# A transformer layer on one core: each feed-forward weight's rounding queued behind the evictions of the product just ended

## The chip, the cores and the metric

The kernel runs on one core of one Trainium2 chip. The metric is the device time of one execution in microseconds (us), here the median of several runs. A core has four engines that compute and that each work through a queue of their own, in order: TensorE (PE in the profile, with its weight loads as PEld), VectorE (DVE), ScalarE (ACT) and GpSimd (POOL). SyncE (SP), ACT and POOL also issue DMAs. [...]

## The reference, cut to what matters

The reference is one trunk layer for 640 tokens (128 of context, 512 of a latent grid) with 1024 features: adaLN modulation, two attentions, a gated merge, then a feed-forward, then a last norm. All of it is float32. The change lies in the feed-forward alone:

```
h2 = rmsnorm(x, n2) * (1 + sc2) + sh2
x  = x + g2 * (square(relu(h2 @ w1)) @ w2)      # w1: 1024 x 4096, w2: 4096 x 1024
y  = rmsnorm(x, final_norm_g)
```

## The kernel before, in words

**Number format.** PE multiplies in fp32r, a rounded float32. To keep the precision, an operand is split into a rounded part (hi) and the rest (lo), and a product of two operands is three matmuls: hi by hi, hi by lo, lo by hi. Making hi and lo from a float32 weight is what the change calls the weight's rounding.

**Feed-forward.** Features lie on the partitions, tokens on the free axis. The 4096 hidden features are taken in four chunks (c = 0 to 3). Each layer of a chunk is a 2 by 2 block product, which is done with seven block products in place of eight (a scheme of the Strassen kind, named A11, A12, S3, S2, A22, S1, S4). Layer 1 of chunk 0 is done plainly before. What is left is the list SEQ (line 1368) of 196 products, which the loop at line 1665 goes through. Here they are numbered 0 to 195: chunk 0 has 0 to 27 (layer 2 only), chunk 1 has 28 to 83, chunk 2 has 84 to 139, chunk 3 has 140 to 195. In chunks 1 to 3 the first 26 products are layer 1, then layer 2 follows with two layer-1 products left among it. One product is twelve matmuls of 128x128 by 128x320 (lines 1679 to 1681; only line 1681 reads the lo half of the weight) into one PSUM bank of eight. A12 accumulates onto the bank of A11, and S1 and S4 onto that of S2, after the earlier content has been read.

**After each product** come its evictions (`layer1`, line 1507, and `layer2`, line 1579). In layer 1: ACT copies A11 (line 1510); DVE adds or subtracts S3, A22, S2, S1 and S4 (lines 1514 to 1524); after A12, S2, S1 and S4 ACT does relu and square (lines 1504, 1505), for the last three on what DVE has just written. In layer 2 DVE adds the gated product to the residual `x` (line 1532, in one or two token pieces), after an ACT copy for A11 (lines 1583, 1593). In chunk 3 `done_half` follows for the halves that are then complete: ACT squares `x` (line 1547), DVE adds the square to a sum (line 1551), ACT scales `x` by the last norm's gain (line 1552). When all eight blocks of a half are done, the last norm follows (lines 1559 to 1569) with the output DMAs. Besides there is the work between the layers: `operand` (lines 1482 to 1489) rounds the hidden activations into hi (ACT) and lo (DVE), and `t_raw` (lines 1491 to 1501, DVE) forms their sums and differences.

**Weights.** `Operands.feed` (line 1387) loads a float32 weight pair into a staging buffer, through the SP queue (line 1398). There are three buffers for the A products (`wst`) and four for the others (`wsb`), and the latter get a second weight block added by an accumulating DMA from the POOL queue (line 1401). `Operands.conv` (line 1409) is the rounding of the next product's weight: hi by ACT (line 1416), lo by DVE (line 1421; by POOL for A12 and A22 of layer 1; for the four S4 of chunk 3 by an ACT copy of -hi, line 1418, and an accumulating DMA from POOL, line 1419). After S3, S2 and A22 it has POOL add the next block into the same staging half (line 1424); after A12 and S4 the staging buffer is free and `feed` loads the next into it. `wb` has six buffers, three each under two tags in turn, so a weight's rounding can start when the product six places before it has ended. `ahead` (line 1432) calls `conv` at the end of each product's code, so the weight of product i+6 is rounded in the code of product i.

**Order.** The program is traced in the order of the code. A list scheduler then lays down each engine's queue: at each step it takes, of the instructions that are ready by its own reckoning, the one traced first. So the rounding for product i+6, traced after the evictions of product i, can still be laid ahead of them where it is ready sooner. The queues so laid are fixed: on the chip an instruction that waits holds up all behind it.

Of the kernel before, what the change touches and what calls it, by code (L numbers as in the profile page):

```python
# [74 lines left out]
def trunk_layer(ctx: ExitStack, tc: tile.TileContext, xT, small_in, wmodA, wmodB, tabs, cacheK, cacheV, bias,  # L75
                w_in, w_br, w_out, w1, w2, yT, akT, avT, bkT, bvT):
    nc = tc.nc
    PE, ACT, DVE = nc.tensor, nc.scalar, nc.vector
# [154 lines left out]
    def flush_later(todo=None):  # L233
        todo = later if todo is None else todo
        n = len(todo)
        for f in todo[:n]:
            f()
        del todo[:n]

    class Weights:  # L240
        def __init__(self):
            self.order = list(w_order())
            self.pos = {k: i for i, (k, _) in enumerate(self.order)}
            self.st, self.t = {}, {}
            self.nd = self.nc = self.live = self.busy = 0
            self.extra = self.defer = False
            self.behind = None
# [51 lines left out]
        def ahead(self):  # L299
            while self.nc < len(self.order):  # L300
                key = self.order[self.nc][0]
                if key in EXTRA and self.extra:
                    return
                if key not in EXTRA and self.live + 2 > 6:
                    return
                self.conv()
            if OPS:
                OPS[0].ahead()

    OPS = []  # L310
# [1059 lines left out]
    class Operands:  # L1370


        def __init__(self):
            self.st = {}
            self.loads = []
            for l, c, n, o in SEQ:
                k = (l, c, n, "A" if o in ("A11", "A12") else "B")
                if k not in self.loads:
                    self.loads.append(k)
            self.t = {}  # L1380
            self.nl = self.nc = 0
            self.busy = {"A": 0, "B": 0}

        def src(self, l, c, n, e):
            return (w1[8 * c + 2 * n + e] if l == 1 else w2[c, 2 * n + e]).rearrange("p (k n) -> p k n", k=KT)
# [46 lines left out]
        def ahead(self):  # L1432
            self.feed()
            while self.nc < len(SEQ) and W.live < 6 and (SEQ[self.nc][0], *SEQ[self.nc][1:3],
                                                         "A" if SEQ[self.nc][3] in ("A11", "A12") else "B") in self.st:
                self.conv()

        def get(self, x):
            while x not in self.t:
# [5 lines left out]
    def bank():  # L1445
        return pp8[0].tile([P, 512], F32, tag="b", bufs=8, name="b")[:, :HT]
# [22 lines left out]
    def opd(c, name):  # L1469
        if (c, name) not in OPD:  # L1470
            OPD[c, name] = (bp[0].tile([P, 8, HT], F32R, tag="op3", bufs=1, name="op") if len(OPD) % 3 == 2 else
                            m.tile([P, 8, HT], F32R, tag="op", bufs=2, name="op"))
        return OPD[c, name]
# [6 lines left out]
    def operand(c, name, ks=slice(0, 4)):  # L1480

        t, src = opd(c, name), hid_raw(c, {"B11": 11, "B21": 21, "T4": 21, "N22": 22}.get(name, 12))[:, ks]
        hi, lo = t[:, ks], t[:, 4 + ks.start:4 + ks.stop]
        if name == "N22":
            ACT.activation(hi, src, AF.Copy, scale=-1.0)
            DVE.scalar_tensor_tensor(lo, src, -1.0, r32(hi), op0=OP.mult, op1=OP.subtract)
        else:
            ACT.activation(hi, src, AF.Copy)  # L1488
            DVE.tensor_sub(lo, src, r32(hi))  # L1489

    def t_raw(c, name, ks=slice(0, 4)):

        b11, b12, b21, b22 = (hid_raw(c, b)[:, ks] for b in (11, 12, 21, 22))
        if name == "T3":
            DVE.tensor_sub(b12, b22, b12)
        elif name == "T2":
            DVE.tensor_add(b12, b12, b11)
        elif name == "T4":
            DVE.tensor_sub(b21, b21, b12)
        else:  # L1500
            DVE.tensor_sub(b12, b22, b12)
# [72 lines left out]
    def fold(n):  # L1574

        for h in range(2):
            gate_half(2 * n + 1, WS[n], h, neg)
# [58 lines left out]
    for n, h in todo:  # L1636
# [7 lines left out]
        e, i = n % 2, n // 2  # L1644
# [20 lines left out]
    for x in SEQ:  # L1665
        l, c, n, o = x
        w = OPS[0].get(x)
        if l == 1:
            xk = XN[o]
        else:  # L1670
            s = opd(c, XOF[o])
            xk = lambda k, s=s: (s[:, k], s[:, 4 + k])
        p = pairs.setdefault((l, c, n), Pair())
        whole = {"A12": "A11", "S1": "S2", "S4": "S2"}.get(o)
        b = getattr(p, "b" + whole) if whole else bank()
        setattr(p, "b" + o, b)
        for k in range(4):
            xh, xl = xk(k)
            PE.matmul(b, w[:, k], xh, start=not whole and k == 0, stop=False, skip_group_check=True)  # L1679
            PE.matmul(b, w[:, k], xl, start=False, stop=False, skip_group_check=True)  # L1680
            PE.matmul(b, w[:, 4 + k], xh, start=False, stop=o not in ("A11", "S2", "S1") and k == 3, skip_group_check=True)  # L1681
        (layer1 if l == 1 else layer2)(c, n, o, b, p)
        W.live -= 1
        if l == 1 and o in ("A12", "S2") and n > 1:
            operand(c, "B11" if o == "A12" else "B21", slice(0, 3) if n == 2 else slice(3, 4))
        if l == 1 and o == "S2":
            fold(n)
        if l == 1 and o == "S4" and n > 1:
            t_raw(c, "T3", slice(0, 3) if n == 2 else slice(3, 4))
        if l == 2:  # L1690
            if (o, n) == ("A11", 2):
                operand(c, "T3")
                t_raw(c, "T2")
                t_raw(c, "T4")
            if (o, n) == ("A11", 3):
                operand(c, "T4")
            if (o, n) == ("A12", 3):
                operand(c, "T2")
                t_raw(c, "T1")
            if (o, n) == ("S3", 3):  # L1700
                operand(c, "T1")
            if (o, n) == ("S2", 3):
                operand(c, "N22")
        OPS[0].ahead()
        flush_later()
        if side:
            side.pop(0)()
# [104 lines left out]
```

## Time and profile before

| | |
|---|---|
| median of 3 runs | 917.87 us (917.49, 917.87, 919.94) |
| the profiled execution's own time | 917.51 us |
| its span, first to last instruction | 915.7 us |
| DVE busy | 713.5 us, 78% of the span |
| ACT busy | 564.8 us, 62% |
| POOL busy | 197.0 us, 22% |
| granted TensorE clock, mean | 0.997 |

A row of a timeline has: start in us, duration in us, engine, line, operation, what it writes and reads, and in square brackets the idle time of the engine ahead of it with what ended it. A row of waits has: engine, what waited, `<-` what it waited for, then us in total, how many times, and the longest. A row of a table of windows has: the stretch, its length, then busy us of PE, PEld, DVE, ACT and POOL with the numbers of instructions, then the granted clock, the DMA share and GB/s. The chain of work that ended last has: start, duration, what.

### The profile page before, as it was taken

The numbers are of one execution on the slowest core, as the hardware profiler recorded it, in microseconds if no ns is written. First come the engines' busy times: TensorE is split into PE (matmuls) and PEld (weight loads), VectorE is DVE, ScalarE is ACT, GpSimd is POOL, SyncE is SP. The second block draws the span as 40 slices with busy tenths as digits, with TensorE's granted clock in tenths as the row PEclk, the third lists the DMA queues.
The fourth block names the chain that finished last, engine by engine and source line by source line (L and its number), as shares of the span: only waits on it lengthen the run. The fifth ranks groups of instructions, "written<-read, shape, count | busy, mean of one in ns | idle before, by whom it ended". The sixth has DMA issues, their size and how long they took to land.

```text
span 915.7 us, 16620 instructions
## 1 busy us (share of the span) xinstructions
PE 901.5 (98%) x6120; PEld 871.5 (95%) x6120; DVE 713.5 (78%) x1508; ACT 564.8 (62%) x1176; POOL 197.0 (22%) x226
## 2 busy tenths in 40 slices
PE   9999999999999999999999999999999999999996
PEld 7799989999999999999999999999999999999995
DVE  6776887757666796767789996995798769976897
ACT  4566777756667765765325667537753576357765
POOL 0020200001211011211120000354244532454140
PEclk9999999999999999999999999999999999999998
DMA  9892400126645398999743463898778876898475
GB/s 348 317 266 69 113 24 26 62 72 159 161 119 125 120 284 256 249 268 251 251 140 100 116 165 105 134 210 186 186 122 191 178 174 144 180 173 182 97 126 151
DMA packets 54465, 151.09 MB, mean 165 GB/s; under 512 B 6704, under 2 KB 10432, under 8 KB 54384
## 3 DMA queue, kind: packets, MB, share of 16 engines
q1 hardware_dynamic: 31440, 99.74, 33.1%
q0 software_dynamic: 21792, 48.98, 30.8%
q10 hardware_dynamic: 1152, 1.31, 0.4%
q8 instruction: 48, 0.79, 0.4%
q14 instruction: 33, 0.27, 0.1%
HBM read 137.67 MB, written 4.60 MB: 155 GB/s over the span
## 4 chain that ended last, share of the span: by engine, by line
PE 81%; DVE 6%; DMA 5%; ACT 4%; issue 2%; POOL 0%; SPq 0%; DVEq 0%; ACTq 0%; POOLq 0%
PE b L1680 10%; PE b L1679 10%; PE b L1681 10%; PE pg L320 7%; PE pg L321 7%; PE pg L322 7%; PE pss L322 4%; PE pss L321 4%; PE pss L320 4%; DMA wsb<-w 2%; PE pt L321 2%; PE pt L322 2%; PE pt L320 2%; DMA ms<-wmodA 2%; PE pt L710 1%
## 5 line engine op out<-in xcount | busy, mean ns | idle before, releaser
L1416 ACT ACTIVATE wb<-wsb 128x512 fp32r<-128x512 f32 x140 | 87.1, 628 | 90.6 <-PE b L1681 59.2
L1680 PE MATMUL b<-op,wb 128*128 128x320 f32 x448 | 138.6, 309 | 0.7 <-DVE op L1489 0.7
L1679 PE MATMUL b<-op,wb 128*128 128x320 f32 x448 | 138.6, 309 | 0.0
L1681 PE MATMUL b<-op,wb 128*128 128x320 f32 x448 | 138.4, 309 | 0.0
L1421 DVE TENSOR_TENSOR wb<-wsb,wb 128x512 fp32r<-128x512 f32 x124 | 92.5, 749 | 26.5 <-ACT wb L1416 26.3
L1424 POOL DMA_DIRECT2D wsb<-w x84 | 74.4, 922 | 127.8 <-DVE wb L1421 99.7
L1123 DVE SCALAR_TENSOR_TENSOR mt<-wmt,cb 128x512 f32<-128x512 f32 x128 | 80.9, 686 | 6.0 <-DMA wmt<-wmodB 6.0
L1680 PEld LDWEIGHTS b<-op,wb 128*128 128x128 f32 x448 | 84.1, 188 | 1.2 <-DVE op L1489 1.2
L1679 PEld LDWEIGHTS b<-op,wb 128*128 128x128 f32 x448 | 84.1, 188 | 0.5 <-DVE x L1532 0.4
L1681 PEld LDWEIGHTS b<-op,wb 128*128 128x128 f32 x448 | 84.1, 188 | 0.0
L272 ACT ACTIVATE wh<-wst 128x512 fp32r<-128x512 f32 (+1 forms) x84 | 61.1, 739 | 32.1 <-PE pg L321 16.6
L1401 POOL DMA_DIRECT2D wsb<-w x28 | 26.0, 930 | 138.0 <-DVE xm L341 41.5
L281 DVE TENSOR_TENSOR wl<-wst,wh 128x512 fp32r<-128x512 f32 (+1 forms) x53 | 43.3, 821 | 14.9 <-ACT wh L272 12.8
L648 DVE TENSOR_TENSOR pl<-pt,ph 128x512 fp32r<-128x512 f32 (+1 forms) x72 | 44.9, 627 | 11.8 <-ACT ph L647 11.2
L647 ACT ACTIVATE ph<-pt 128x512 fp32r<-128x512 f32 (+1 forms) x72 | 39.2, 548 | 15.7 <-PE po L718 4.7
L1532 DVE SCALAR_TENSOR_TENSOR x<-b,parts,x 128x128 f32<-128x128 f32 (+1 forms) x116 | 46.3, 429 | 2.9 <-PE b L1681 2.2
L1416 ACT ACTIVATE wb<-wst 128x512 fp32r<-128x512 f32 x56 | 34.9, 626 | 17.1 <-PE b L1681 10.3
L1679 PE MATMUL b<-t,wb 128*128 128x320 f32 x144 | 44.7, 310 | 0.0
L1681 PE MATMUL b<-t,wb 128*128 128x320 f32 x144 | 44.5, 309 | 0.0
L1680 PE MATMUL b<-t,wb 128*128 128x320 f32 x144 | 44.5, 309 | 0.0
L1489 DVE TENSOR_TENSOR op<-hid,op 128x1280 fp32r<-128x1280 f32 (+2 forms) x32 | 37.0, 1155 | 7.6 <-ACT op L1488 7.4
L1532 DVE SCALAR_TENSOR_TENSOR x<-tp,parts,x 128x320 f32<-128x320 f32 (+2 forms) x60 | 38.9, 677 | 1.0 <-ACT tp L1583 1.0
(890 smaller groups left out, 3009.2 us busy)
## 6 DMA issues: line engine op xcount, KB each, us to landing
wsb<-w POOLq DMA_DIRECT2D x112, 256.0 KB, 5.1
wst<-w SPq DMA_DIRECT2D x36, 512.0 KB, 3.9
wmt<-wmodB SPq DMA_DIRECT2D x32, 512.0 KB, 5.5
wst<-w_in SPq DMA_DIRECT2D x31, 512.0 KB, 4.4
wsb<-w SPq DMA_DIRECT2D x28, 512.0 KB, 4.0
ms<-wmodA SPq DMA_DIRECT2D x16, 512.0 KB, 8.2
wl<-w_in POOLq DMA_DIRECT2D x10, 512.0 KB, 7.6
wst<-w_br SPq DMA_DIRECT2D x8, 512.0 KB, 4.2
```

What stands on the lines that cost most here:

```text
L272: ACT.activation(hi[:, ks], st[:, ks], AF.Copy)
L320: PE.matmul(ps, wh[:, k], xh[:, sl], start=first, stop=False)
L321: PE.matmul(ps, wh[:, k], xl[:, sl], start=False, stop=False)
L322: PE.matmul(ps, wl[:, k], xh[:, sl], start=False, stop=last)
L1123: DVE.scalar_tensor_tensor(t, st[:, q * 512:(q + 1) * 512], 1.0, r32(cb[2 * q + i][:, :512]), op0=OP.mult, op1=OP.mult, accum_out=parts[:, ...
L1416: ACT.activation(w[:, 0:4], t, AF.Copy)
L1421: (nc.gpsimd if o in BLKPOOL[l - 1] else DVE).tensor_sub(w[:, 4:8], t, r32(w[:, 0:4]))
L1424: nc.gpsimd.dma_start(t, self.src(l, c, n, e)[:, 4 * half:4 * half + 4], accum_op=OP.add)
L1532: DVE.scalar_tensor_tensor(X1[i][:, sl], src[:, sl.start - off:sl.stop - off], g[:, j:j + 1], X1[i][:, sl], op0=OP.mult, op1=OP.add)
L1679: PE.matmul(b, w[:, k], xh, start=not whole and k == 0, stop=False, skip_group_check=True)
L1680: PE.matmul(b, w[:, k], xl, start=False, stop=False, skip_group_check=True)
L1681: PE.matmul(b, w[:, 4 + k], xh, start=False, stop=o not in ("A11", "S2", "S1") and k == 3, skip_group_check=True)
```

## The change

After the evictions of each product the loop notes the last instruction traced so far on ACT and the last on DVE. When `ahead` then rounds a weight, each of its ACT instructions is queued behind the noted ACT instruction, and each of its DVE instructions behind the noted DVE instruction. These are bounds on the order in the queue and no waits. Instructions on POOL and SP get no such bound. Products whose evictions have no ACT instruction note an older one. The roundings are traced where they were, six products ahead; the first six are traced ahead of the loop and have no bound.

```diff
@@ class Operands, __init__
             self.busy = {"A": 0, "B": 0}
+            self.behind = []
@@ ahead
-                self.conv()
+                with ExitStack() as order:
+                    for i in self.behind:
+                        order.enter_context(tc.issue_after(i))
+                    self.conv()
@@ the loop over SEQ
         (layer1 if l == 1 else layer2)(c, n, o, b, p)
+        OPS[0].behind = [next(i for i in reversed(nc.cur_bb.bb.instructions) if i.engine == e.engine) for e in (ACT, DVE)]
         W.live -= 1
```

## The prediction

> **What bounds the kernel now.** I read the page first, then a table of windows over the feed-forward, then what PE waited for, then the timelines of PE, ACT and DVE around each wait and at the end.
>
> ```profile
> span 915.7 us, 16620 instructions
> PE 901.5 (98%) x6120; PEld 871.5 (95%) x6120; DVE 713.5 (78%) x1508; ACT 564.8 (62%) x1176; POOL 197.0 (22%) x226
> ```
> ```profile
> 713.00:766.00 53.00, 52.57 (x359) 52.31 (x358) 37.63 (x61) 36.75 (x73) 19.31 (x19) 1.00 0.77 182
> 859.00:906.00 47.00, 47.00 (x316) 46.27 (x315) 44.83 (x84) 35.53 (x66) 13.86 (x16) 1.00 0.57 94
> ```
>
> PE is busy for 98% of the span, at the full granted clock. The first window is layer 1 of chunk 2: 359 matmuls in 52.57 us are 0.146 us each, so a product of twelve takes 1.76 us. The second is layer 2 of chunk 3: DVE is busy 44.83 of 47 us (95%) and has hardly any room. So only the places where PE stands still can be won. In the feed-forward these are few:
>
> ```profile
> PEld b L1679 <- DVE tp L1518: 0.5, 2, 0.3
> ```
> ```profile
> 752.47 0.31 PE L1679 MATMUL b<-op,wb 128*128 128x320 f32 x1
> 753.21 0.42 PE L1680 MATMUL b<-op,wb 128*128 128x320 f32 x1 [0.43 <-DVE op L1489]
> 753.46 0.31 PE L1681 MATMUL b<-op,wb 128*128 128x320 f32 x1
> ...
> 852.19 0.31 PE L1679 MATMUL b<-op,wb 128*128 128x320 f32 x1
> 852.78 0.41 PE L1680 MATMUL b<-op,wb 128*128 128x320 f32 x1 [0.28 <-DVE op L1489]
> ```
>
> From start to start, 752.47 to 753.46 is two steps that should take 0.29 us and take 0.99: 0.70 lost, of which 0.10 is the slow step behind the wait. At 852.19 it is 0.59 - 0.15 + 0.10 = 0.54. The two waits for L1518 (at 820 and 840) make 0.5 together. That is 1.74 us in all, 0.19% of 917.5: more than that cannot be won in the products.
>
> **The change, part by part.** No instruction is added or taken away and nothing waits that did not; only places in the queues of ACT and DVE change. Where the order changes is seen in a pattern that all 36 S2, S1 and S4 products of layer 1 have in common:
>
> ```profile
> 835.00 0.63 ACT L1416 ACTIVATE wb<-wst 128x512 fp32r<-128x512 f32 x1 [0.81 <-PE b L1681]
> 835.53 0.46 ACT L1504 ACTIVATE hid<-tp 128x320 f32<-128x320 f32 x1
> 836.02 0.47 ACT L1505 ACTIVATE hid<-hid 128x320 f32<-128x320 f32 x1
> ```
>
> The rounding starts when the product ends (835.00), while DVE still makes `tp`; relu and square come behind. Bound, ACT waits for DVE (0.48 us, the duration of L1518 below), does relu and square (0.49 + 0.47 from start to start and in duration) and rounds then: 1.4 us later, and DVE's lo half by as much. Relu and square come 0.5 us earlier. A weight is needed six products or 10.5 us on, which hides 1.4 us; in layer 2 of chunks 0 to 2 the evictions are DVE's but for A11's copy, they already stand ahead of the rounding, and nothing changes.
>
> **First gain: the hand-over from layer 1 to layer 2.** PE waits at 752 and 852 for an operand's lo half, which comes out of this chain (the first row is its place in chunk 2, the others in chunk 3):
>
> ```profile
> 749.07 0.63 ACT L1416 ACTIVATE wb<-wsb 128x512 fp32r<-128x512 f32 x1 [2.04 <-DMA wsb<-w]
> ...
> 848.64 0.63 ACT L1416 ACTIVATE wb<-wsb 128x512 fp32r<-128x512 f32 x1 [1.58 <-DMA wsb<-w]
> ...
> 851.37 0.47 ACT L1488 ACTIVATE op<-hid 128x320 fp32r<-128x320 f32 x1
> ```
> ```profile
> 852.24 0.48 DVE L1489 TENSOR_TENSOR op<-hid,op 128x320 fp32r<-128x320 f32 x1
> ```
>
> ACT stood still until 848.64 for a staging DMA, with the rounding for product 169 at the head of its queue and relu and square of product 163 behind it. Bound, those two are done before that wait and no longer stand in the chain. But the DMA itself was set off by a rounding and is up to 1.4 us later: rounding done at 850.67, then relu, square and L1488 of product 164 (0.49 + 0.47 + 0.47) at 852.1, L1489 at 852.6 at the latest; each of these steps overlaps the one before it by some 0.1. PE wants it at 852.34, one step after 852.19. So of 0.54 some 0.2 may stay; from 749.07 the same steps give 752.5 to 753.0 against 752.62, and 0.2 of 0.70. I take 0.70 + 0.54 - 0.4 = 0.85 won (0.4 to 1.24).
>
> **Second gain: two waits for L1518.** The one at 840:
>
> ```profile
> 838.40 0.63 ACT L1416 ACTIVATE wb<-wsb 128x512 fp32r<-128x512 f32 x1 [1.21 <-DMA wsb<-w]
> 838.94 0.46 ACT L1505 ACTIVATE hid<-hid 128x320 f32<-128x320 f32 x1
> 839.43 1.01 ACT L1488 ACTIVATE op<-hid 128x960 fp32r<-128x960 f32 x1
> ```
> ```profile
> 839.07 0.69 DVE L1421 TENSOR_TENSOR wb<-wsb,wb 128x512 fp32r<-128x512 f32 x1 [2.71 <-ACT wb L1416]
> 839.68 0.48 DVE L1518 TENSOR_TENSOR tp<-tp,b 128x320 f32<-128x320 f32 x1
> ```
>
> The rounding for product 163, which a staging DMA made late, holds ACT at 838.40, its lo half holds DVE at 839.07, and L1518, the eviction of product 158, is behind that; PE wants its bank. Bound, the rounding comes behind L1505 of product 157, and L1488, which is traced before it and ready with L1505, goes ahead as well. By the scheduler's reckoning the lo half is then ready 0.47 + 0.47 + 1.01 + 0.63 = 2.6 us after product 157, and L1518 after 1.76: L1518 is laid first. The 0.25 is won. At 820 a lo half also stood ahead of an eviction: 0.25. Should L1518 stay behind, it is a loss (a rival below).
>
> How long those accumulating DMAs take is the size that decides here. All 84 of them:
>
> ```profile
> DMA to landing us min/median/max: 3.9/4.9/9.0
> ```
>
> [...]
>
> **The loss: the end.** In chunk 3 the evictions of S2 and S1 run through `done_half`, whose ACT part waits for a DVE that is several us behind PE. The rounding was free of that; bound, it is not.
>
> ```profile
> 889.64 0.68 DVE L1421 TENSOR_TENSOR wb<-wsb,wb 128x512 fp32r<-128x512 f32 x1
> 890.24 0.67 DVE L1532 SCALAR_TENSOR_TENSOR x<-tp,parts,x 128x128 f32<-128x128 f32 x2
> ```
> ```profile
> 891.52 0.46 ACT L1547 ACTIVATE sq<-x 128x320 f32<-128x320 f32 x1
> 892.00 0.56 ACT L1552 ACTIVATE x<-x,pk 128x320 f32<-128x320 f32 x1
> 892.47 0.61 ACT L1416 ACTIVATE wb<-wsb 128x512 fp32r<-128x512 f32 x1
> 892.99 0.62 ACT L1418 ACTIVATE wb<-wsb 128x512 fp32r<-128x512 f32 x1
> 893.51 0.46 ACT L1547 ACTIVATE sq<-x 128x320 f32<-128x320 f32 x1
> ```
> ```profile
> 895.88 0.86 POOL L1419 DMA_DIRECT2D wb<-wsb  x1 [0.88 <-PE b L1681]
> ```
> ```profile
> DMA to landing us min/median/max: 3.3/3.3/3.7
> ```
> ```profile
> 904.07 0.31 PE L1681 MATMUL b<-op,wb 128*128 128x320 f32 x1
> ```
>
> DVE gets to the gated add of product 184 (the first S2) at 890.24; bound, the lo half at 889.64 comes behind it, so the add runs from 889.64 to 890.3. From there ACT has six products in lockstep (184 to 189): the starts give 0.48 for the square, 0.47 for the scaling, 0.52 for hi, 0.52 for -hi (the four S4 weights only), so 6 x 1.47 + 4 x 0.52 = 10.9 us, and the last copy is done at 901.3. Today it is done before the DMA at 895.88, which lands by 899.6: a slack of 4.5 us. Now that DMA starts at about 901.6 and lands 3.3 to 3.7 later, at 905.0 to 905.3. The last product wants the weight's second half at 904.07: a loss of 0.9 to 1.2, up to 1.5 with the gaps in which ACT waits for DVE. I take +1.2, with 0 as the lower end (DVE gets to the adds earlier and ACT starts sooner) and +5.0 as the upper (below). The close behind the last product stays as it is: it hangs on the last eviction, not on a rounding.
>
> **The sum.** -0.85 - 0.25 - 0.25 + 1.2 = -0.15. Against the profiled execution's 917.51 that is 917.36; the median of the runs lies 0.36 above that execution, so 917.7. 0.3% of the time, about what a measurement of this kernel can tell from no change, is 2.75 us.
>
> **The rivals.**
>
> The gains without the loss: the end keeps its slack of 4.5 us. For it speaks that a weight is traced 10.5 us ahead; against it that ACT's 10.9 us at the end leave no room. Then -1.24 - 0.5 = -1.74, or 916.1. Chance 0.14.
>
> It does next to nothing: the bound exchanges neighbours whose order PE never feels, and DMAs still set the waits. For it speaks that layer 2 of chunks 0 to 2 keeps its order; against it that the waits at 752 and 852 hang on the exchanged order. Time 917.9, chance 0.10.
>
> The staging chain takes the gain's place: L1421 stays ahead of L1518 at 839.07, and the DMA that it waits for is 1.4 us later because the rounding that set it off is. Then PE waits 1.4 us longer at 840. In chunk 2 the same place has some room:
>
> ```profile
> 739.47 0.48 DVE L1518 TENSOR_TENSOR tp<-tp,b 128x320 f32<-128x320 f32 x1
> ```
> ```profile
> 740.59 0.31 PE L1679 MATMUL b<-t,wb 128*128 128x320 f32 x1
> ```
>
> L1518 ends at 739.95 and PE wants the bank at 740.59: of 1.4 us 0.64 is covered and 0.75 lost. -0.85 - 0.25 + 1.4 + 0.75 + 1.2 = 2.25, or 920.1. Chance 0.10.
>
> ACT and DVE in turn, slower: at the end each product's gated add (0.67) is laid on DVE behind the lo half or the sum of the one before, so that ACT stands still for it six times. ACT's chain is then 10.9 + 6 x 0.67 = 14.9 us, ends at 905.3, the last DMA lands at 909.1, and the loss at the end is 5.0 in place of 1.2: 3.65 in all, or 921.5. It is beyond 2.75 us from a loss of 4.1 at the end. For it speaks a DVE busy for 95%; against it that DVE has the adds of several products to do while ACT works off one. Chance 0.12.
>
> The clock: PE stands so long in one place that it is slowed.
>
> ```profile
> 907.17 0.81 PE L1559 MATMUL b<-sq,ones 128*128 128x320 f32 x2 [0.39 <-ACT sq L1547]
> ```
> ```profile
> 911.00:912.00 1.00, 0.00 (x0) 0.00 (x0) 1.00 (x4) 0.00 (x0) 0.00 (x0) 0.53 1.02 350
> ```
>
> PE's last matmuls end at about 908, and the granted clock is at a half from 911 on: some 3 us of standing still. No single wait above is over 1.5 us. If one reached 3 us, it would cost that and about as much for the work at half clock behind it, some 6 us: 924. Chance 0.02. [...]
>
> **How the numbers follow.** The forecast has 0.52; its own range, from the ends of its terms, is 917.0 (-1.24 - 0.5 + 0.9) to 918.7 (-0.4 - 0.25 + 1.5). The gains alone reach down to 916.1, the staging chain up to 920.1 and the slower rival to 921.5. 916.0 to 921.0 leaves out most of that last one, the clock and little else, some 0.15. Faster by over 2.75 us needs more than PE stands still for in all: 0.03. Slower by over 2.75 us is the last two rivals and a part of the staging chain with gaps: 0.15. The rest, 0.82, is within.
>
> **What would show it.** Right: L1416 behind L1505 after S1, S2 and S4; no wait of PE for L1489, or a quarter of it, at the two hand-overs; L1518 ahead of L1421 and no wait for it near 840; PE waiting for `wb` or its DMA in the last four products, 1.2 us in all. Wrong: PE's waits for L1489 unchanged, a longer wait for L1518, no wait at the end, or PE waiting for weights in the middle of a layer.

## The result and the profile after

The time rose from 917.68 us (median of 4 runs, the three above and one of 915.68) to 927.66 us (4 runs: 926.5, 927.17, 928.15, 929.4). The medians differ by 10.0 us; the ratio on record is 1.0102, 95% interval 1.0085 to 1.0120, which is 9.4 us slower. The prediction was 917.7 with a range up to 921.0. Two disturbed executions among the experiments (1250.55 us of `quiet`, 2266.41 us of `s42_only`) stand in the medians, but not in the ratios. The profiled execution of the changed kernel took 928.15 us. Lines are up to four higher than before: the rounding is 1417 (hi) and 1422 (lo), the staging transfers 1402 and 1425, relu and square 1508 and 1509, the operand 1492 and 1493, the evictions 1518 to 1528, the matmuls 1683 to 1685; at the end the gated add is 1536, the square of `x` 1551 and its scaling 1556, the copy of -hi 1419 and its DMA 1420, the last norm's matmuls 1563.

The head of the page and, from the list of what PE waited for, the rows of the feed-forward (the last fence is the row of before that answers to them):

```profile
span 926.4 us, 16616 instructions
PE 906.9 (98%) x6120; PEld 873.8 (94%) x6120; DVE 708.2 (76%) x1508; ACT 561.8 (61%) x1176; POOL 195.6 (21%) x226
```
```profile
PE b L1685 <- DMA wb<-wsb: 1.6, 1, 1.6
PE b L1683 <- ACT op L1492: 1.4, 3, 0.6
PE b L1684 <- DVE op L1493: 1.1, 3, 0.4
PE b L1683 <- DVE tp L1522: 0.6, 2, 0.4
PE b L1685 <- DVE wb L1422: 0.2, 1, 0.2
```
```profile
PE b L1680 <- DVE op L1489: 0.7, 2, 0.4
```

DVE, ACT and POOL have no more work than before, and PE has the same 6120 matmuls. PE's busy time grew by 5.4 us and its idle time by 5.3: a matmul of 0.31 us overlaps the next, which starts 0.147 later, so a pause shows in part as busy time, and at the end some matmuls are slower (below). Losses are therefore taken from start to start here. Before, the operand cost PE two waits of 0.7 us in all. Now both of its halves cost it waits, three times each, once in every one of chunks 1 to 3, and a weight's DMA at the end comes on top.

Where the 10.7 us of longer span (926.4 - 915.7) arose is read from the start of each product in the two timelines. The shift of after against before is 0.72 at the first product of the loop and at product 28 (this comes from ahead of the loop, where the two programs are the same, and differs from one execution to the next: from -0.3 to 3.1 us in the runs below), 2.83 at product 84, 4.14 at 140, 5.70 at 172, 6.33 at 188, 9.94 behind the last product. So layer 1 with its hand-overs lost 2.1 in chunk 1, 1.3 in chunk 2 and 1.6 in chunk 3, layer 2 of chunk 3 lost 0.6, the last products 3.6, and the close 0.8.

The hand-over of chunk 2, which stood at 752.47 before:

```profile
755.37 0.31 PE L1685 MATMUL b<-op,wb 128*128 128x320 f32 x1
756.26 0.41 PE L1683 MATMUL b<-op,wb 128*128 128x320 f32 x1 [0.59 <-ACT op L1492]
757.03 0.42 PE L1684 MATMUL b<-op,wb 128*128 128x320 f32 x1 [0.36 <-DVE op L1493]
757.29 0.31 PE L1685 MATMUL b<-op,wb 128*128 128x320 f32 x1
```

From 755.37 to 757.29 is three steps of 0.147 that took 1.92: 1.48 lost, and 0.10 in a slow step behind it, 1.58 in all. It was 0.70 before. The same sum at the other two gives 1.29 (none before) and 1.53 (0.54 before).

What lies behind the first of these, in chunk 1, is seen in the chain of waits from 630 to 657 us (columns: start, duration, what):

```profile
by line: DMA wsb<-w 54.7%; issue 13.1%; ACT wb L1417 6.9%; DVE wb L1422 6.7%; ACT op L1492 3.7%; ACT hid L1509 3.5%; ACT hid L1508 3.0%; POOL wsb L1402 2.2%; DVE op L1493 2.0%; DVE tp L1522 1.8%; DVE tp L1525 1.5%; PE b L1684 1.5%; PE b L16
...
642.46 0.49 DVE tp L1522
...
642.98 0.48 ACT hid L1508
...
643.48 0.47 ACT hid L1509
...
644.38 1.00 ACT op L1492
...
646.80 0.68 DVE wb L1422
647.48 0.41 DVE tp L1525
...
648.09 5.15 DMA wsb<-w
...
653.33 0.63 ACT wb L1417
...
```

The same view of the kernel before, 630 to 654 us, names nothing but PE:

```profile
by line: PE b L1680 33.7%; PE b L1681 33.5%; PE b L1679 33.1%
```

Before, PE followed PE without a gap; after, more than half of the stretch hangs on transfers into `wsb`. (At the other two hand-overs PE waited before too, and the chain behind it hung on the same transfers for 40.5% of 740 to 753.7 us and 65.7% of 835 to 853 us.) The transfer at 648.09 is where the change enters. Before, the lo half that empties its block, the transfer and the rounding of what it brought stood thus in the timelines of DVE, POOL and ACT:

```profile
642.97 0.97 DVE L1421 TENSOR_TENSOR wb<-wsb,wb 128x512 fp32r<-128x512 f32 x1 [0.74 <-ACT wb L1416]
643.86 1.16 DVE L1489 TENSOR_TENSOR op<-hid,op 128x960 fp32r<-128x960 f32 x1
```
```profile
644.24 0.88 POOL L1424 DMA_DIRECT2D wsb<-w  x1 [0.85 <-DMA wsb<-w]
```
```profile
649.24 0.63 ACT L1416 ACTIVATE wb<-wsb 128x512 fp32r<-128x512 f32 x1 [0.80 <-PE b L1681]
```

And after:

```profile
645.40 1.47 DVE L1493 TENSOR_TENSOR op<-hid,op 128x960 fp32r<-128x960 f32 x1 [1.39 <-ACT op L1492]
646.80 0.68 DVE L1422 TENSOR_TENSOR wb<-wsb,wb 128x512 fp32r<-128x512 f32 x1
```
```profile
648.09 0.86 POOL L1425 DMA_DIRECT2D wsb<-w  x1 [0.68 <-DVE tp L1525]
```
```profile
653.33 0.63 ACT L1417 ACTIVATE wb<-wsb 128x512 fp32r<-128x512 f32 x1 [0.78 <-DMA wsb<-w]
```

The lo half and the operand's lo part have changed places on DVE. The operand waits for its hi part on ACT, that one stands behind relu and square and one more rounding, and relu waits for an eviction on DVE; the rounding whose lo half is seen here now stands behind them all. Its transfer is issued 3.85 us later (648.09 against 644.24; the profile names the eviction L1525, right behind the lo half, as what released it), 2.5 more than PE is late by then (1.37 at product 54). Before, the rounding at 649.24 found its data there (the profile names PE, which freed the buffer); at 653.33 it waits for the transfer, with relu, square and the operand of the hand-over behind it on ACT. The transfers themselves did not become much slower: from issue to landing at least 3.9, median 5.3, at most 8.2 us, where before it was 3.9, 4.9 and 9.0.

**The end.** The timelines of ACT, POOL and PE:

```profile
897.46 0.47 ACT L1551 ACTIVATE sq<-x 128x320 f32<-128x320 f32 x1 [6.13 <-DVE x L1536]
...
901.62 0.47 ACT L1551 ACTIVATE sq<-x 128x320 f32<-128x320 f32 x1 [1.09 <-DVE x L1536]
...
908.82 0.61 ACT L1419 ACTIVATE wb<-wsb 128x512 fp32r<-128x512 f32 x1
```
```profile
904.03 0.87 POOL L1420 DMA_DIRECT2D wb<-wsb  x1 [9.76 <-PE b L1685]
...
909.73 0.86 POOL L1420 DMA_DIRECT2D wb<-wsb  x1 [0.39 <-PE b L1685]
```
```profile
905.52 0.30 PE L1684 MATMUL b<-op,wb 128*128 128x320 f32 x1
907.39 0.41 PE L1685 MATMUL b<-op,wb 128*128 128x320 f32 x1 [1.56 <-DMA wb<-wsb]
```
```profile
904.00:908.00 4.00, 2.41 (x12) 1.59 (x11) 2.35 (x6) 3.97 (x10) 1.73 (x2) 1.00 0.54 94
908.00:912.00 4.00, 4.00 (x19) 4.00 (x18) 0.95 (x2) 4.00 (x10) 1.72 (x2) 0.57 0.76 130
```

ACT runs the six products in lockstep as forecast, from 897.46 to 909.43, 12.0 us. The first of the four DMAs that add up a lo half is issued at 904.03, and PE waits for it in product 192, which takes 4.06 us from start to start, 2.2 more than before. From 908.37 to 911.81 PE's matmuls then start 0.27 apart in place of 0.147 (the window from 908 on has a granted clock of 0.57), and product 193 takes 1.4 us more than before.

### The profile page after: what moved, and what is told of

The parts are those of the page before. It is cut to its first block, busy times and chain, and to the rows that moved or that the text cites. A ratio compares the mean times of both kernels' runs of the same rounds, so it can differ in the third digit from the quotient of the medians.

```text
span 926.4 us, 16616 instructions
## 1 busy us (share of the span) xinstructions
PE 906.9 (98%) x6120; PEld 873.8 (94%) x6120; DVE 708.2 (76%) x1508; ACT 561.8 (61%) x1176; POOL 195.6 (21%) x226
## 4 chain that ended last, share of the span: by engine, by line
PE 74%; DVE 8%; DMA 8%; ACT 5%; issue 4%; POOL 1%; SPq 0%; ACTq 0%; DVEq 0%; POOLq 0%
PE b L1683 8%; PE b L1685 8%; PE b L1684 8%; PE pg L320 7%; PE pg L321 7%; PE pg L322 7%; DMA wsb<-w 6%; PE pss L322 4%; PE pss L321 4%; PE pss L320 4%; PE pt L321 2%; PE pt L322 2%; PE pt L320 2%; PE pt L710 1%; ACT wb L1417 1%
## 5 line engine op out<-in xcount | busy, mean ns | idle before, releaser
L1422 DVE TENSOR_TENSOR wb<-wsb,wb 128x512 fp32r<-128x512 f32 x124 | 89.0, 723 | 26.9 <-ACT wb L1417 26.9
L1422 DVE TENSOR_TENSOR wb<-wst,wb 128x512 fp32r<-128x512 f32 x44 | 29.9, 689 | 17.7 <-ACT wb L1417 17.4
L1508 ACT ACTIVATE hid<-tp 128x320 f32<-128x320 f32 x36 | 17.0, 471 | 37.0 <-DVE tp L1525 14.4
```

Source lines behind the costliest of these rows:

```text
L1422: (nc.gpsimd if o in BLKPOOL[l - 1] else DVE).tensor_sub(w[:, 4:8], t, r32(w[:, 0:4]))
```

## The experiments

Two theories were set against each other. **Staging**: a bound rounding that issues a transfer issues it later, and the weight behind that transfer is late. **In turn**: a bound rounding holds up the small operations laid behind it on ACT and DVE, whatever it issues. Each run of the kernel before was on the same chip as the runs that it is compared with.

**Which engine's bound.** `act_only` and `dve_only` keep one of the two bounds.

```diff
- for e in (ACT, DVE)]
+ for e in (ACT,)]      # act_only; dve_only: (DVE,)
```

> Only the roundings' hi halves on ACT are bound, DVE's lo halves are free. In-turn theory (ACT now stands for DVE's evictions, DVE then for ACT's hi halves): the loss stays, 8 to 10 us over the kernel before. Rival, DVE's bound is to blame (lo halves leave their places): within 2 us of the kernel before. The theory that later roundings make later staging DMAs says 8 to 10 as well.

> Only the lo halves on DVE are bound, ACT's hi halves are free. In-turn theory: within 1 us of the kernel before. Rival, DVE's bound is to blame: 8 to 10 us over it.

Measured: 926.96 against 918.22, ratio 1.0097 (1.0081 to 1.0113), and 919.66 against 918.22, 1.0008 (0.9993 to 1.0023). ACT's bound alone makes nearly the whole loss. That was to be expected of either theory: the lo half follows the hi half anyway.

**Which products.** `not_last` leaves out the last chunk's layer 2, `last_only` binds there alone.

```diff
- for e in (ACT, DVE)]
+ for e in (ACT, DVE)] if (l, c) != (2, 3) else []   # not_last; last_only: ==
```

> Bound as in the changed kernel, but not behind the layer-2 products of chunk 3 (those with the last norm's work in their evictions). The trace after has a shift of 5 us up to product 170, 0.7 of it ahead of the loop, and 4.5 behind. If the two losses are separate: 4 to 5.5 us over the kernel before, no half clock in the last products. If the end only pays for what came late from layer 1: 8 to 10. If all of it arises at the end: under 1.

> Bound only behind the layer-2 products of chunk 3. If the two losses are separate: 3.5 to 5.5 us over the kernel before, with PE waiting some 3 us for the last four weights and a half clock for some 3 us. As the prediction sized the end: 1.2. If it needs the lateness from layer 1: under 1.

Measured: 925.01, 1.0079 (1.0059 to 1.0099), and 925.09, 1.0075 (1.0050 to 1.0100). Both medians lie over what was expected of two separate losses (4 to 5.5 and 3.5 to 5.5), and their differences add up to 13.7 us, more than the 10.0 of the change. The traces of the places in question do add up: `not_last` loses 5.7 over the loop (shift 0.65 at its start, 6.37 at its end), `last_only` 3.5 in the last four products, together 9.2, and the change loses 9.2 (0.72 to 9.94). What `last_only` has beyond that lies elsewhere: 3.1 at the start of the loop and 1.6 up to product 166 (mostly at the waits near 840), both ahead of its bound, and 0.4 in layer 2 before the last products; its four runs lie at 923.3 and 926.8, in two pairs. So both parts are real, and a median of four runs of it is good to some 2 us only.

**Without the accumulating staging transfers.** `before_nodma` and `after_nodma` leave out line 1424 (1425).

```diff
             if o in ("S3", "S2", "A22"):
                 e, half = {"S3": (1, 1), "S2": (0, 1), "A22": (1, 0)}[o]
-                nc.gpsimd.dma_start(t, self.src(l, c, n, e)[:, 4 * half:4 * half + 4], accum_op=OP.add)
+                pass
```

> The kernel before without the accumulating DMAs that follow a rounding (line 1424 of the kernel before), so the S2, S1 and S4 weights are taken from the wrong blocks. It is the partner of the next run. All theories: 0 to 2 us under the kernel before, since its waits at the hand-overs and for the eviction of S2 (1.7 us) hang on those DMAs.

> The changed kernel without the same DMAs (line 1425 there), so the S2, S1 and S4 weights are taken from the wrong blocks. Staging theory (the bound roundings set off their DMAs later, and ACT and DVE stand behind what waits for them): the loss in layer 1 goes, what stays is the end, so 3 to 5 us over its partner. In-turn theory (ACT and DVE hold each other up without any DMA): the loss stays, 8 to 10 us over its partner.

Both leave out work, and S2, S1 and S4 get other weights, so these two are for the time alone. Measured: 916.3 against 918.38, 0.9975 (0.9966 to 0.9985), and 922.7, 1.0050 (1.0035 to 1.0065). Without these transfers the change costs 6.4 by the medians, more than the 3 to 5 expected of staging and less than the 8 to 10 of in turn. In the traces the loss from product 28 to 188 falls from 5.6 to 0.3 (shift 1.15 to 1.46; against its partner, whose waits at 752, 820, 840 and 852 all vanished, it is 2.3), of which some 0.5 us is lost around each of the three hand-overs. The end keeps 3.1. So, each version against its partner, the accumulating transfers carry 3.3 of the 5.6 us ahead of the last products, and next to nothing of the end.

**Only S2, S1 and S4 of layer 1, or only A11 and A12.** The prediction's pattern on ACT belongs to the first group.

```diff
- for e in (ACT, DVE)]
+ for e in (ACT, DVE)] if l == 1 and o in ("S2", "S1", "S4") else []   # s_only; a_only: ("A11", "A12")
```

> Bound only behind S2, S1 and S4 of layer 1, whose relu waits for DVE. If these make the loss in layer 1: 4.5 to 7 us over the kernel before, like the run that leaves out the end. If A11 and A12 make it, whose evictions ACT reads from PSUM itself: under 1.5.

> The bound only behind the products A11 and A12 of layer 1. If all of layer 1's loss is at the S products, whose following roundings stand before the operand of the hand-over and issue the transfers: within 1 us of the kernel before (0.5 us lower if the roundings laid between relu's operations were what held up the stores). If roundings are late wherever they are bound: 2 to 4 us slower.

Measured: `s_only` 927.48 against 918.38, 1.0097 (1.0082 to 1.0112), over the 4.5 to 7 us expected; `a_only` 917.57 against 918.14, 0.9994 (0.9981 to 1.0008). All of layer 1's loss is behind S2, S1 and S4, and it is larger alone than with the rest. What PE waited for in `s_only`, and the head of its chain of waits from 630 to 659.3 us, the hand-over of chunk 1:

```profile
PE b L1683 <- ACT op L1492: 3.8, 3, 1.5
PE b L1683 <- DVE tp L1522: 3.4, 3, 2.1
```
```profile
by line: DMA wsb<-w 74.9%; ACT wb L1417 6.1%; POOL wsb L1402 5.0%; DVE wb L1422 4.8%; issue 4.5%; DVE op L1493 1.7%; ACT op L1492 1.6%; PE b L1684 1.4%; ACT hid L1509 1.3%; ACT hid L1508 1.1%; POOLq L1402 0.3%; POOLq L1425 0.1%; ACTq L1417 
```

PE names an operand and an eviction as what it waited for. Neither is slow; three quarters of the chain behind them is one staging transfer after another. `a_only` sets a limit to the staging theory: of the 24 roundings that it binds, six products ahead, 15 set off an accumulating transfer or free a buffer for a load, and they cost nothing. Behind A11 and A12 ACT reads the bank itself and doesn't wait for DVE. What a rounding issues is not enough; it must also be laid behind an eviction that waits.

**The roundings that issue transfers against those that don't.** Both bind outside the last chunk's layer 2. `loud` binds only roundings of weights other than A11's and S1's (S3, S2 and A22 issue an accumulating transfer, A12 and S4 free a buffer and so issue the next loads); `quiet` binds only the roundings of A11 and S1, which issue nothing.

```diff
-                    for i in self.behind:
+                    for i in self.behind if SEQ[self.nc][3] not in ("A11", "S1") else []:   # loud; quiet: in
```

> The bound on the roundings outside the last chunk of layer 2, and there only on those whose weight is not that of A11 or S1 (these are the roundings that issue the next staging transfer or free a buffer for one). Staging theory (a rounding laid later issues its GpSimd transfer later, and the weight behind it is late): nearly the whole loss of the kernel bound everywhere but in the last chunk stays, 5 to 7.3 us, and the waits at the hand-overs of layer 1 (products 54, 110, 166) stay at over 1 us each, ended by a transfer into wsb. In-turn theory (a bound rounding holds up the small operations that the factorization laid behind it on ScalarE and VectorE, whatever it issues): the loss goes with the number of bound roundings, about 5 of 7 of it, 4 to 5 us.

> The other part of the same kernel: outside the last chunk of layer 2, the bound only on the roundings of the weights of A11 and S1, which issue no transfer. Staging theory: within 1 us of the kernel before, and no wait of PE ended by a late weight or operand that was not there before. In-turn theory: 2 of 7 of the loss, 1.5 to 2.5 us, as waits of 0.3 to 0.6 us at the hand-overs of layer 1 that no transfer ends.

Measured: `loud` 928.72 against 918.14, 1.0114 (1.0082 to 1.0145); `quiet` 917.11, 0.9991 (0.9974 to 1.0008). The whole loss ahead of the last chunk's layer 2 is with the roundings that issue transfers or free a buffer for one. `quiet` is a fair test of the other theory, for 15 of the 36 roundings that `s_only` binds are also bound in it, behind S1 and S4 with their relu and square. The in-turn theory wanted 1.5 to 2.5 us of `quiet`, and its interval ends at 0.7. First the waits of `loud`, then those of `quiet` (558 to 917 us), then the heads of their chains up to the hand-over of chunk 1:

```profile
PE b L1683 <- DVE tp L1522: 4.6, 5, 1.5
PE b L1683 <- ACT op L1492: 1.8, 2, 1.2
```
```profile
PE b L1563 <- ACT sq L1551: 0.8, 1, 0.8
PE b L1683 <- DVE tp L1522: 0.4, 1, 0.4
```
```profile
by line: DMA wsb<-w 58.6%; issue 11.9%; ACT wb L1417 6.7%; ACT op L1492 5.0%; ACT hid L1509 3.5%; ACT hid L1508 3.0%; DVE wb L1422 2.6%; POOL wsb L1402 2.1%; DVE op L1493 2.0%; DVE tp L1522 1.8%; DVE tp L1525 1.5%; PE b L1684 1.5%; ACTq L14
```
```profile
by line: PE b L1683 34.1%; PE b L1685 33.5%; PE b L1684 33.3%
```

`loud` costs more than the 5 to 7.3 us expected and more than `not_last` (10.6 against 6.8 us), which binds the same roundings and others; so does `s_only` (9.1). Binding the harmless roundings too seems to give a part back. Why is open.

**PE kept busy at the end.** `last_warm` is `last_only` with 14 matmuls more ahead of product 192, so that PE does not stand idle before the first late weight.

```diff
+        if (l, c, o, n) == (2, 3, "S4", 0):
+            d = bank()
+            for _ in range(14):
+                PE.matmul(d, prev[0][:, 0], prev[1](0)[0], start=True, stop=True, skip_group_check=True)
```

> Bound only behind the layer-2 products of chunk 3, with 14 extra matmuls (2.05 us at full clock) ahead of the first of the last four products, whose result nothing reads: they fill a part of PE's wait for the weights. If the waits alone make the loss at the end: as the run without the extra matmuls or up to 1 us over it (925.1 to 926). If the half clock behind the waits has a share: no half clock, and 1 to 2 us under it (923 to 924).

Measured: 922.72, 1.0053 (1.0038 to 1.0068). Its window from 904 to 908, then two of `last_only`:

```profile
904.00:908.00 4.00, 4.00 (x27) 3.61 (x26) 2.48 (x5) 4.00 (x11) 1.38 (x2) 1.00 0.78 134
```
```profile
904.00:908.00 4.00, 2.43 (x10) 2.17 (x11) 1.08 (x3) 4.00 (x9) 1.66 (x2) 0.82 0.77 133
908.00:912.00 4.00, 4.00 (x23) 4.00 (x22) 1.76 (x4) 3.60 (x10) 0.93 (x2) 0.76 0.77 131
```

The clock stays full, and the loss from product 184 on is 3.0 (shift 1.61 to 4.65) against 3.5. The 2.4 us between the medians is no measure of it, for the trace has 3.4 us of difference at the start of the loop already. So the half clock is worth about 0.5 us of the end; the late weights are the rest. The slow steps themselves take more (in the changed kernel 13 steps, 0.12 too long each, 1.5 us), but PE would else wait for a later weight. `after_nodma` shows it, whose clock stays full as well, behind a wait as long as that of the changed kernel:

```profile
900.00:904.00 4.00, 2.40 (x15) 1.89 (x14) 1.48 (x4) 4.00 (x10) 1.29 (x3) 1.00 0.76 131
904.00:908.00 4.00, 3.56 (x23) 3.09 (x22) 2.48 (x5) 4.00 (x11) 1.32 (x2) 1.00 0.77 131
```

There PE waits for a second one of these DMAs (0.44 us, at 906.96), and its end loses 3.1.

**Is there a gain at the hand-over at all?** `s42_only` binds behind three products only, the S4 of block 2 in each chunk, with whose evictions the first operand of the hand-over is made. `quiet_s42` joins it with `quiet`. The trace is that of `s42_trace`, the same kernel as `s42_only`.

```diff
- for e in (ACT, DVE)]
+ for e in (ACT, DVE)] if (l, o, n) == (1, "S4", 2) else []
```

> The bound only behind the S4 products of block n=2 of layer 1, three products in the run, so that only the rounding ahead of the hand-over's first operand is laid behind the evictions. If the prediction's gain is there when the staging chain is left alone: the waits at 752 and 852 us shrink from 0.70 and 0.54 towards 0.2, and the time is 0.5 to 1.2 us lower. If the one rounding suffices to hold up its transfer as in the change: waits of about 1.2 to 1.6 us at two or three hand-overs, 1 to 3 us slower.

> Outside the last chunk of layer 2, the bound on the roundings of the weights of A11 and S1, and on whichever roundings stand behind S4 of block n=2 of layer 1. If the gain predicted at the hand-over is real and separate from what the harmless roundings bring: 1.5 to 2.2 us below the kernel before, and the waits at the products 54, 110 and 166 at 0.2 us or less. If it is one gain, that of stores which no rounding stands before: 0.8 to 1.2 us below. If both were noise: within 0.5 us, with waits of 0.5 us at 110 and 166 as in the kernel before.

> The kernel of s42_only once more, for its trace. If the gain is at the hand-over: the waits at the products 110 and 166 are each 0.4 us or less where the kernel before has 0.70 and 0.54. If it is not: they are at 0.5 us or more, and the difference of the times lay in the spread.

Measured: `s42_only` 917.08 against 918.14, 0.9988 (0.9975 to 1.0001); `quiet_s42` 917.19 against 918.11, 0.9987 (0.9977 to 0.9998). In `s42_trace` (918.59 in its one run) PE passes product 110 without a gap and loses 0.30 at 166; 0.70 and 0.54 before. The gain of 0.94 is there, at these two places. The loop as a whole is no shorter in that execution (shift 0.98 at its start, 1.07 at its end): a wait of 0.7 us stands at 624 and the one near 840 is longer by 0.7. The hand-over of chunk 2 in `quiet_s42`:

```profile
753.14 0.34 PE L1683 MATMUL b<-op,wb 128*128 128x320 f32 x1
753.32 0.31 PE L1683 MATMUL b<-t,wb 128*128 128x320 f32 x1
753.59 0.41 PE L1684 MATMUL b<-op,wb 128*128 128x320 f32 x1
```

Here the scheduler also laid a step of the next product (`t`) into the wait, and 0.24 is lost at each of the three hand-overs. The two gains do not add: it is one gain of about 1 us (0.2 to 2.1 by the interval). `quiet_s42` is a little faster than the kernel before, and the only version here that leaves nothing out and whose interval stays below 1, barely.

## Why the prediction was wrong, step by step

**Right.** ACT got the order that was forecast: the rounding behind relu and square. At the end ACT ran in lockstep, as forecast, with no turn-taking for each of the six products. The wish for a gain at the hand-over was sound too: 0.85 was predicted, and 0.94 is found at those two places in `s42_trace`, where only three roundings are bound. (They are those of S4 weights, which free a buffer; once in a chunk, that costs nothing.)

**Right by luck: the wait near 840.** It is gone, but not as forecast. The prediction had the operand's hi part go ahead of the rounding and the eviction of product 158 ahead of the lo half. Here are ACT and DVE:

```profile
842.69 0.64 ACT L1417 ACTIVATE wb<-wsb 128x512 fp32r<-128x512 f32 x1 [0.25 <-DMA wsb<-w]
843.23 0.99 ACT L1492 ACTIVATE op<-hid 128x960 fp32r<-128x960 f32 x1
```
```profile
843.36 0.69 DVE L1422 TENSOR_TENSOR wb<-wsb,wb 128x512 fp32r<-128x512 f32 x1 [1.02 <-ACT wb L1417]
843.97 0.48 DVE L1522 TENSOR_TENSOR tp<-tp,b 128x320 f32<-128x320 f32 x1
```

The rounding still stands ahead of the operand, and its lo half ahead of the eviction. The rounding starts 4.29 us later than before (838.40), while PE is 4.53 late; these 0.24 us cover the wait. The other wait, at 820, grew from 0.25 to 0.65.

**Wrong: "the DMA itself was set off by a rounding and is up to 1.4 us later".** This step decides the result. It took the displacement from the plain pattern, a rounding that changes places with relu and square. Ahead of a hand-over `operand` is traced there as well, in pieces of 128x960 with 1.00 on ACT and 1.15 to 1.47 on DVE. Once the rounding stands behind relu, the operand goes ahead of it too, and behind it on DVE follows the lo half that empties the block: 3.85 us later, 2.5 of it beyond PE's own shift. The prediction had such a displacement before it: at 840 it has L1488 go ahead, adds it up to 2.6 us and counts the result as a gain. The exchange came about at the next operand and not at that one, and the prediction did not put the same 2.6 into a transfer.

**Wrong: "a weight is needed six products or 10.5 us on, which hides 1.4 us".** That holds for the weight that is rounded late. It does not hold for the weight that is staged into the block it leaves. That one passes through rounding, transfer (5.15 us) and rounding again, several times in a chunk, and each late link makes the next late. `quiet` against `loud` shows it: the roundings that issue nothing are hidden, as the step says (-1.0 us, interval -2.4 to 0.7); with the others the cost is 10.6. So at the hand-overs the two waits of 0.70 and 0.54 did not shrink to 0.4 in all but became three of 1.29, 1.58 and 1.53: 3.2 us of the 5.6 that are lost ahead of the last products. The rest is spread over smaller waits.

**The rival "the staging chain takes the gain's place" had the mechanism**, at a chance of 0.10 and 920.1 us, but named one place, L1518 near 840, where it cost nothing. The chain acts wherever a staging transfer hangs on a bound rounding.

**The end: the mechanism was right, the size not.** Predicted +1.2, measured 3.6. From product 184, where the shift is 6.12, ACT's chain should have begun at 890.4 of before's time; it began at 891.3 (897.46 - 6.12), 0.9 later. It should have lasted 10.9 us and lasted 12.0, of which 1.09 is one gap in which ACT waited for an add that DVE had laid behind lo halves. That makes 1.2 + 0.9 + 1.1 = 3.2, near what `last_warm` and `after_nodma` lose with a full clock (3.0 and 3.1); the half clock, about 0.5 by `last_warm`, gives the rest. The prediction reckoned with the last weight; PE met the lateness at the first of the four, product 192.

**The clock.** "No single wait above is over 1.5 us. If one reached 3 us" was the wrong question. The longest one was 1.87 us from start to start (905.52 to 907.39), and the clock went to a half all the same (0.50 from 908.40 to 911.81), behind a stretch of 4 us in which PE was busy for 2.41. It did so in `last_only` too (1.88 us; busy for 2.43). But in `after_nodma` (1.88 us; 2.40) it stayed at 1.00, and `s_only` has a like place at 656 to 660 us (1.80 us; 2.40) and a mean clock of 0.997, as the kernel before (the changed kernel and `last_only` have 0.996). So neither figure decides by itself, and what does is open. The cost put on a wait of 3 us, as much again for the work at half clock, was the author's estimate, and no run shows it: the half clock here lasted 3.41 us and was worth about 0.5 us (`last_warm`).

**Left open.** Without the accumulating transfers of line 1425, 2.3 of the 5.6 us stay lost, some 0.5 us around each hand-over among them; whether the first loads (with their own accumulating DMAs, line 1402) or the order of the operand cause it was not separated. Nor is it known why fewer bounds (`s_only`, `loud`) cost more than `not_last`, which has theirs and others.

## What to carry to other kernels

Before a step is moved in a queue, list what it issues, and follow each transfer to the work that needs it: slack belongs to the datum, and the datum staged into the freed buffer has less of it than the one just made. Where an order is bounded, work out the displacement at the place with the most work traced ahead, not at the typical one; a part of the bounded places can make the whole loss. If such a bound is wanted, put it on the steps that issue nothing, or behind work that does not wait, and on the one place where it helps.

## What the runs showed of the hardware

In the changed kernel TensorE's granted clock fell to a half (0.57 over the window from 908 to 912) behind a stretch of 4 us in which PE was busy for 2.41, without a pause of over 1.87 us; behind 2.40 busy of 4 and a pause of 1.88 us in `after_nodma` it stayed at 1.00, and so it did in `last_warm` (3.40 busy of the 4 us from 900). The half clock lasted 3.41 us (0.50 from 908.40 to 911.81); the two windows of `last_only` (0.82 and 0.76 of 4 us each) make about 3.4 us of half clock. The accumulating transfers of 256 KB into `wsb` took 3.9 to 9.0 us from issue to landing (median 4.9 before, 5.3 after), those between `wb` and `wsb` 3.3 to 3.7. The time ahead of the feed-forward, where all programs are the same, differed by up to 3.4 us between executions, more than several of the effects asked for; the shift of product starts from one place to another told more than the medians did, though single waits (that near 840 above all) come and go between versions too.
